# Hybrid mLSTM / gated-DeltaNet / HGRN2 step: the prompt's tokens first, then sample, then meta tokens, with fewer and narrower score and update matmuls

## The chip, the cores and the metric

The kernel runs on one core of one Trainium2 chip. The metric is device time in microseconds (us) of one execution. Five engines work from their own in-order queues: TensorE (PE in the profile, its weight loads PEld), VectorE (DVE), ScalarE (ACT), GpSimd (POOL), and SyncE (SP), which here issues every DMA.

## The reference

One layer of a decoder. A sequence of 1024 prompt tokens with 16 learned meta tokens ahead of it, and 8 sample sequences of 8 tokens, go through one wide projection; 16 heads of three kinds mix the tokens; a gated, head-normalised result goes through the output projection. The meta tokens are dropped from the output, but they leave a state behind (and a convolution history) on which the prompt goes on.

```python
proj = einsum('bld,de->ble', rmsnorm(x), w_in)      # 2048 -> 8984 columns
(aq, ak, av, ao, ai, af, bq, bk, bv, ba, bb, cq, cf, ci, z) = split(proj)
# 6 mLSTM heads (A), 6 gated-delta heads (B, with a width-4 convolution over q, k, v), 4 HGRN2 heads (C)
# HGRN2, inside a chunk: A[t,s] = sum_d q[t,d] k[s,d] exp(b[t,d] - b[s,d]),  s <= t, b = cumsum(log f)
#   o = (q exp(b)) S + A v ;  S' = exp(b_end) S + (k exp(b_end - b))^T v
y = concat(ha, hb, hc) * rsqrt(mean(.^2) + eps) * out_norm_w * silu(z)
out = x + einsum('ble,ed->bld', y, w_out);  y_prompt = rmsnorm(out[:, 16:]) * final_norm_w
```

Every float is 32 bits wide, and all states are outputs: those of the prompt, and those of the 8 sample sequences.

## The kernel before

**Two halves.** The tokens lie along the free axis. The first half (class `Half`, index 0) has 592 columns: 64 of the samples (`NSAMP`), 16 meta (together `NT0` = 80), and the first 512 of the prompt; the second half has the other 512. The normalised, transposed input is kept as pairs hi, lo of rounded floats (`hT`, tiles hA and hB in the profile); so is each piece of weights (`feed_split`: ACT makes `whi`, DVE makes `wlo` from `wraw`). A product is whi·hi + whi·lo + wlo·hi.

**Projection.** A head has 4 or 5 column tiles of 128 columns (`head_tiles`: q, k, v, the output gate o of an A head, z, and f of a C head). For each tile `run_group` goes over 16 blocks of the inner dimension, 3 products each; in the first half every product is two matmuls of 296 columns (`half.accs`, 592 / 2), in the second one of 512. The results are the tiles `acc`. All token columns are computed for every tile, those of the meta tokens too.

**Everything else is woven between these matmuls.** `Weave` holds queues of generators (scan, fin, post, bg); after each inner step `pump` lets those go on whose due time, by a table of assumed instruction costs (`Clock`), has come. Where a queue must be empty, at a new head or at the end of a half, `drain` runs the generators with no projection in between. The recorded program then passes a scheduler that also moves instructions on each engine.

**Heads.** `gate_scan` and `gates` make the gate rows of all A and B heads, write them to DRAM and read them back per head. `mlstm_scan`, `gdn_scan` and `hgrn_scan` work by chunks of 128 prompt tokens (`main`) and one small group of the 80 sample and meta tokens. In `hgrn_scan`, `score` fills the chunk's matrix `AT` level by level: first the diagonal (kT against qT), then for each block length hh of 1, 2, 4, 8 one matmul per chunk (tile `pa`) whose wanted entries a mask picks with a predicated copy; the last level takes hh = 16 for the whole chunk and puts hh = 32 and 64 over it with small matmuls of 32x32 and 64x64 (tile X of level 32, tile Ex of level 64). `sample_update` adds 8 outer products to the sample states of a head: keys as hi and lo (`kq`, 64 + 64 rows), values `vh` and `vl` spread by a row mask to 4 x 128 columns (`vx`), two matmuls of 512 columns (tile `pu`) for each half of the 8 sequences. In the first half `conv_evac` and `conv_post` load the 24 old rows of a B tile (tile `cr`), transpose them on PE (tile `pch`) and copy them into the convolution's input U, for each of the 18 tiles.

**Start.** `prep` normalises and transposes tiles of tokens: 0 (sample and meta, 80 rows), 1 and 2 (128 prompt rows each) ahead of the first matmul, 3 and 4 in the background of the first pass, which computes the first 296 columns of two tiles.

Of the kernel before, what the change touches and what calls it, by code (L numbers as in the profile page):

```python
# [28 lines left out]
WB = HALF  # L29
SUB = 16  # L30
# [16 lines left out]
class Half:  # L47
    def __init__(self, index):
        self.index = index
        self.first = index == 0  # L50
        self.width = WA if self.first else WB
        self.base = NT0 if self.first else 0
        self.tiles = ([(0, NT0)] if self.first else []) + [(self.base + P * c, P) for c in range(NC)]
        self.accs = [(0, WA // 2), (WA // 2, WA // 2)] if self.first else [(0, WB)]
        n0 = len(self.tiles) - NC
        self.main = Group(P, NC, self.base, n0, False)
        self.groups = ([Group(NT0, 1, 0, 0, True)] if self.first else []) + [self.main]
# [123 lines left out]
def hybrid_step(ctx, tc, i, o):  # L181
# [98 lines left out]
    def new_accs(half, cols):  # L280
        return [[bank("acc") for _ in half.accs] for _ in cols]

    def run_group(half, cols, accs, parts, after=None):
        for g in range(NG):
            for n in range(len(cols)):
                whi, wlo = next_piece()
                for q in range(4):
# [5 lines left out]
                    for w, part, first, last in products:  # L293
                        for a, (off, cnt) in list(zip(accs[n], half.accs))[parts]:
                            T.matmul(a[:, 0:cnt], w[:, cs], hT[g][part][:, q, off:off + cnt], start=first, stop=last)
# [6 lines left out]
    def spans(half, acc):  # L302
        return [(a[:, 0:cnt], off, cnt) for a, (off, cnt) in zip(acc, half.accs)]
# [49 lines left out]
    def load_x(n):  # L353
        xs = [row(("eghj" if n in (2, 3) else "abcd")[g], f"x{g}")[:, 0:512] for g in range(NG)]
# [32 lines left out]
    def prep(tiles):  # L387
        pend = []
        for n in tiles:
            cnt, col = (P, NT0 + P * (n - 1)) if n else (NT0, 0)  # L390
            xs = xtiles.pop(n) if n in xtiles else load_x(n)
            pend.append((xs, prep_stats(xs, cnt, n > 1), cnt, col, n > 1))
# [8 lines left out]
    xtiles = {0: load_x(0)}  # L401
# [8 lines left out]
    xtiles.update({n: load_x(n) for n in (1, 2)})  # L410
# [25 lines left out]
    xtiles.update({n: load_x(n) for n in (3, 4)})  # L436
# [5 lines left out]
    first_accs = new_accs(halves[0], first_cols)  # L442
# [85 lines left out]
    G.tensor_copy(imask, ident)  # L528
    rowmask = cp.tile([P, NB], F32, name="rowmask")
# [23 lines left out]
    hist = cp.tile([P, 3 * HB, 3], F32, name="hist")  # L553

# [58 lines left out]
    def gate_scan(half, acc):  # L613

        both = row("c", "both")
        for a, off, cnt in spans(half, acc):
            S.copy(both[:, off:off + cnt], a)
# [6 lines left out]
        for _, off, cnt in spans(half, acc):  # L624
# [6 lines left out]
    def gates(half, pre, li):  # L631
# [65 lines left out]
        DMA(rd[R_NM], M[RF])  # L697
        DMA(rd[R_EM], em[RF])
# [17 lines left out]
        for n, (c0, cnt) in enumerate(half.tiles):  # L716
# [39 lines left out]
    def finish(half, head, outs, ssq, scale, zs):  # L756
# [28 lines left out]
        for part, t in enumerate((yhi, ylo)):  # L785
            t = t.bitcast(F32)
            at_ = 2 * NSAMP if half.first else 0
            DMA(d[:, at_ + HALF * part:at_ + HALF * (part + 1)], t[:, half.base:half.base + HALF])
            if half.first:
                DMA(d[:, NSAMP * part:NSAMP * (part + 1)], t[:, 0:NSAMP])  # L790

    def sample_cols(t):
        return t[:, 0:NSAMP].rearrange("p (b x) -> p b x", x=NS)
# [44 lines left out]
    def sample_update(st, keys, vals, dec, dst, h):  # L838

        st = st[:, :, 0:P]  # L840
        G.tensor_tensor(st, st, dec.unsqueeze(2).to_broadcast([P, NB, P]), op=ALU.mult)
        k2, vl = (sp.tile([P, P], F32R, tag=t, name=t, bufs=1) for t in ("kq", "vl"))
        vh = sq("Wt", "vh", dtype=F32R)
        keys, vals = keys[0:NSAMP], vals[0:NSAMP, 0:P]
        S.copy(k2[0:NSAMP], keys)
        S.copy(vh[0:NSAMP], vals)
        S.copy(vh[NSAMP:P], vals)
        ck.sync()
# [3 lines left out]
        ck.sync()  # L852
# [13 lines left out]
    def mask_rows(half, t, m0, op, fill, strict):  # L866
        if half.first:
            V.tensor_tensor(t[:NT0, 0:NT0], t[:NT0, 0:NT0], m0[:NT0], op=op)
        v = half.main.cols(t)
        causal(v, v, fill, strict, reps=NC)  # L870


    def mlstm_scan(half, h, kT, qT, vT, tho, zs, nm, em, st):
        W = half.width
        mask_rows(half, nm, am0, ALU.add, NEG, False)
# [5 lines left out]
        G.tensor_tensor(qd[:, half.base:W], qT[:, half.base:W], em[:, half.base:W], op=ALU.mult)  # L881
# [44 lines left out]
        for g, kw, v1 in zip(half.groups, kws, v1s):  # L926
            if g.small:
# [6 lines left out]
                V.tensor_tensor(nu, nsv, em[:, NS - 1:NSAMP:NS], op=ALU.mult)  # L934
# [18 lines left out]
        for g, E, kw, v1, og in zip(half.groups, Es, kws, v1s, ogs):  # L953
            n = g.n
            hx = gt("5", g)
            for c0 in range(0, g.nt, 2):
                cs = list(range(c0, min(c0 + 2, g.nt)))
                nd = bank("nd")
                for c in cs:
# [5 lines left out]
                    T.matmul(dst, E[0:n, c, 0:n], v1[0:n, c], start=False, stop=True)  # L965
                ndv = nd[0:n, 0:256 * len(cs)].rearrange("p (c x) -> p c x", x=256)
# [10 lines left out]
            if g.small:  # L977
                upd = sample_update(st, kw[:, 0], v1[:, 0], em[:, NS - 1:NSAMP:NS], o["mC_s"], h)
            yield
            square_sums(g, hx[0:n], ssq)  # L980
# [9 lines left out]
    def conv_evac(half, acc, ei):  # L990
        U = row("u", "U")
        base = NB * (NS + 3)
        if half.first:
            us = U[:, 0:base].rearrange("p (b x) -> p b x", x=NS + 3)
            a0, a1 = acc
# [700 lines left out]
```

## Time and profile before

| what | value |
|---|---|
| median of 3 runs | 2583.55 us (2581.64 to 2584.42) |
| the profiled execution | 2583.26 us, of which the span from first to last instruction is 2581.6 us |
| busy in the span | PE 2525.8, DVE 1352.9, ACT 1010.8, POOL 534.9 us |
| mean granted TensorE clock | 0.994 |
| HBM traffic | 268.93 MB read, 45.42 MB written, 122 GB/s over the span |

The span and the time differ by 1.7 us, which lie outside the instructions. A busy share is a mean over stages; where the engines wait is in the rows further down.

### The profile page before, as it was taken

What the parts mean: (1) busy time and instruction counts of PE and PEld (TensorE: products, weight loads), DVE (VectorE), ACT (ScalarE), POOL (GpSimd) and SP (SyncE); (2) the same over time, 40 slices, a digit from 0 to 9 for tenths busy, and PEclk for the clock granted to TensorE, in tenths of its full rate; (3) what the DMA queues carried; (4) which work ended last, traced back from release to release, by engine and by line L of the source; (5) the groups of instructions that cost most, each with busy time, mean ns of one, the idle gap of its engine ahead of it and who ended that gap; (6) DMA issues with size and microseconds to landing.
All of it is one profiled execution on the core that took longest, in us unless ns stands there. A gap on an engine that the chain in (4) does not pass through costs nothing.

```text
span 2581.6 us, 43090 instructions
## 1 busy us (share of the span) xinstructions
PE 2525.8 (98%) x16084; PEld 2264.0 (88%) x16084; DVE 1352.9 (52%) x2811; ACT 1010.8 (39%) x2423; POOL 534.9 (21%) x665
## 2 busy tenths in 40 slices
PE   6899999999999999999999999999999999999998
PEld 5899999998999999999788888888888888888886
DVE  7664545654645654546764546455454545422435
ACT  5733334342334333334643434333433434322324
POOL 5231212320212321203230103110120101211201
PEclk9999999999999999999999999999999999999999
DMA  5633433555534333435543434334434447535735
GB/s 133 172 82 102 123 81 93 151 142 146 150 87 103 105 108 87 107 92 150 156 112 94 111 85 123 101 96 107 105 91 105 107 99 258 145 85 181 264 98 180
DMA packets 458461, 317.18 MB, mean 123 GB/s; under 512 B 56884, under 2 KB 402572, under 8 KB 457228
## 3 DMA queue, kind: packets, MB, share of 16 engines
q1 hardware_dynamic: 458252, 314.43, 45.1%
q8 instruction: 126, 2.06, 0.3%
q14 instruction: 83, 0.68, 0.1%
HBM read 268.93 MB, written 45.42 MB: 122 GB/s over the span
## 4 chain that ended last, share of the span: by engine, by line
PE 82%; issue 5%; DMA 5%; DVE 3%; POOL 2%; ACT 1%; SPq 1%; POOLq 0%; DVEq 0%; ACTq 0%
PE acc L127 60%; PE oacc L127 8%; PE pa L127 2%; PE pu L127 1%; PE po L127 1%; PE pz L127 1%; PE pyy L127 1%; DMA wraw<-in_w_in_dram 1%; PE nd L127 1%; DMA wraw<-in_w_out_dram 1%; POOL res L127 1%; PE poh L127 1%; POOL X L127 1%; DVE wlo L127 1%; DMA px<-in_x_prompt_dram 1%
## 5 line engine op out<-in xcount | busy, mean ns | idle before, releaser
L127 DVE TENSOR_TENSOR wlo<-wraw,whi 128x512 fp32r<-128x512 f32 x720 | 522.7, 729 | 622.4 <-ACT whi L127 604.8
L127 PE MATMUL acc<-hA,whi 128*128 128x296 f32 x4544 | 837.3, 307 | 8.1 <-ACT whi L127 6.9
L127 ACT CAST whi<-wraw 128x512 fp32r<-128x512 f32 x720 | 443.2, 619 | 937.3 <-PE acc L127 648.4
L127 PE MATMUL acc<-hB,whi 128*128 128x512 f32 x2272 | 722.5, 400 | 0.2 <-ACT whi L127 0.2
L127 PEld LDWEIGHTS acc<-hA,whi 128*128 128x128 f32 x4544 | 683.0, 191 | 16.1 <-ACT whi L127 9.2
L127 PE MATMUL acc<-hA,wlo 128*128 128x296 f32 x2240 | 494.5, 301 | 3.5 <-DVE wlo L127 3.5
L127 PEld LDWEIGHTS acc<-hB,whi 128*128 128x128 f32 x2272 | 408.6, 188 | 77.1 <-ACT whi L127 0.7
L127 PE MATMUL acc<-hB,wlo 128*128 128x512 f32 x1120 | 439.0, 392 | 1.2 <-DVE wlo L127 1.2
L127 PEld LDWEIGHTS acc<-hA,wlo 128*128 128x128 f32 x2240 | 367.4, 190 | 5.4 <-DVE wlo L127 5.3
L127 PE MATMUL oacc<-whi,y 128*128 128x512 f32 x1088 | 344.2, 391 | 0.7 <-ACT whi L127 0.7
L127 PEld LDWEIGHTS acc<-hB,wlo 128*128 128x128 f32 x1120 | 210.2, 188 | 48.9 <-DVE wlo L127 2.8
L127 PEld LDWEIGHTS oacc<-whi,y 128*128 128x128 f32 x1088 | 204.3, 188 | 44.2 <-ACT whi L127 2.4
L127 PE MATMUL oacc<-wlo,y 128*128 128x512 f32 x576 | 224.7, 390 | 0.9 <-DVE wlo L127 0.9
L127 PEld LDWEIGHTS oacc<-wlo,y 128*128 128x128 f32 x576 | 108.2, 188 | 24.5 <-DVE wlo L127 2.5
L127 POOL TENSOR_TENSOR res<-res,fnw 128x512 f32<-128x512 f32 (+1 forms) x34 | 54.3, 1625 | 259.2 <-ACT oscr L127 259.2
L127 POOL TENSOR_TENSOR qd<-qT,emb 128x512 f32<-128x512 f32 x12 | 15.5, 1290 | 361.9 <-PE po L127 288.6
L127 POOL TENSOR_TENSOR vx<-vh,rowmask 128x512 fp32r<-128x512 f32 x32 | 36.1, 1127 | 206.2 <-ACT vh L127 122.5
L127 POOL TENSOR_TENSOR y<-y,zs 128x592 fp32r<-128x592 f32 (+1 forms) x32 | 45.9, 1435 | 139.8 <-ACT zs L127 129.2
L127 DVE TENSOR_TENSOR Yt<-Yc,Bb 128x60 f32<-128x60 f32 (+8 forms) x180 | 36.6, 204 | 44.2 <-DMA Bb<-db 39.1
L127 POOL TENSOR_TENSOR X<-Ex,hk 128x256 f32<-128x256 f32 (+2 forms) x40 | 37.2, 931 | 104.0 <-PE pa L127 90.8
L127 PE MATMUL pa<-X 128*128 128x128 f32 (+2 forms) x480 | 57.8, 260 | 0.5 <-DVE AT L127 0.5
L127 PEld LDWEIGHTS pa<-X 128*128 128x128 f32 (+2 forms) x480 | 50.0, 165 | 9.2 <-issue 0.9
(401 smaller groups left out, 2784.7 us busy)
## 6 DMA issues: line engine op xcount, KB each, us to landing
wraw<-in_w_in_dram SPq DMA_DIRECT2D x564, 256.0 KB
wraw<-in_w_out_dram SPq DMA_DIRECT2D x144, 256.0 KB
y<-y SPq DMA_DIRECT2D x16, 576.0 KB
px<-in_x_prompt_dram SPq DMA_DIRECT2D x32, 256.0 KB
out_dram<-sst SPq DMA_DIRECT2D x16, 512.0 KB
y<-zs SPq DMA_DIRECT2D x32, 256.0 KB
y<-y SPq DMA_DIRECT2D x32, 256.0 KB
res<-in_x_prompt_dram SPq DMA_DIRECT2D x32, 256.0 KB
```

The costliest lines, as they stand in the source:

```text
L127: return f(out, *a, **k)
```

## The change

It does seven things. (1) The columns of the first half are put in the order prompt, sample, meta. (2) Tiles of which the meta tokens need no output (q of A and C heads, o of A heads, all z: 32 of the 71 tiles of the first half) leave the last 16 columns out: two matmuls of 288; the other tiles take 288 and 304. Their 16 columns are set to zero by POOL (`no_meta`). (3) `sample_update` takes four sequences (32 rows) at a time and stacks hi and lo of keys and values as four products in the 128 rows, so that one matmul of 512 columns is left where there were two. (4) `score_near` gets the diagonal and level 1 from one matmul of 192 columns per chunk (kT against `q3`, which holds q of both tokens of a pair and the decayed q of the second). (5) The small group has no level 8 matmul any more. (6) At the last level the four chunk matmuls come first, then the small ones, and those of hh = 64 are two of 32 rows. (7) The old convolution rows come in four loads of 108 rows through a background stream (`load_conv_states`) with four transposes, and POOL copies a tile's part into U. The start takes tiles 1, 2, 3 first, then 4 and 0.

```diff
-        self.accs = [(0, WA // 2), (WA // 2, WA // 2)] if self.first else [(0, WB)]
+    def accs(self, short):
+        if not self.first:
+            return [(0, WB)]
+        return [(0, WS // 2), (WS // 2, (WS if short else WA) - WS // 2)]
...
+        return [[(bank("acc"), off, cnt) for off, cnt in half.accs(what in ("o", "z") or what == "q" and name[0] != "B")]
+                for name, what, _ in group]
...
+    def no_meta(half, t):
+        if half.first:
+            G.memset(t[:, WS:WA], 0.0)
+        return t
...
-    xtiles = {0: load_x(0)}
+    xtiles = {1: load_x(1)}
...
-    for _ in prep([0, 1, 2]):
+    for _ in prep([1, 2, 3]):
...
-    weave.add("bg", prep([3, 4]))
+    weave.add("bg", prep([4, 0]))
...
+    def load_conv_states():
+        rows = 6 * 3 * HB
+        src = i["state_gdn_conv"][0].rearrange("b r (e c) -> (b r e) c", c=P)
+        crs = []
+        for g in range(4):
+            crs.append(sq("cr", "cr"))
+            DMA(crs[g][0:rows], src[rows * g:rows * (g + 1)])
+            ck.last = ck.t["T"] + 4.0
+            yield
+            pc = bank("pch")
+            T.transpose(pc[:, 0:rows], crs[g][0:rows], ident[0:rows, 0:rows])
+            V.tensor_copy(conv_states[:, 6 * g:6 * (g + 1)], pc[:, 0:rows].rearrange("p (q e) -> p q e", e=3 * HB))
...
-        k2, vl = (sp.tile([P, P], F32R, tag=t, name=t, bufs=1) for t in ("kq", "vl"))
-        vh = sq("Wt", "vh", dtype=F32R)
-        S.copy(k2[0:NSAMP], keys)
-        S.copy(vh[0:NSAMP], vals)
-        S.copy(vh[NSAMP:P], vals)
-        V.tensor_tensor(k2[NSAMP:P], keys, k2[0:NSAMP], op=ALU.subtract)
-        V.tensor_tensor(vl[0:NSAMP], vals, vh[0:NSAMP], op=ALU.subtract)
-        V.tensor_tensor(vl[NSAMP:P], vals, vh[0:NSAMP], op=ALU.subtract)
         for part in range(2):
+            rows = slice(32 * part, 32 * (part + 1))
+            k4, v4 = (sp.tile([P, P], F32R, tag=t, name=t, bufs=2) for t in ("k4", "v4"))
+            q = [slice(32 * x, 32 * (x + 1)) for x in range(4)]
+            for x in q[0:2]:
+                S.copy(k4[x], keys[rows])
+            for x in (q[part], q[2]):
+                S.copy(v4[x], vals[rows])
+            for x in q[2:4]:
+                V.tensor_tensor(k4[x], keys[rows], k4[rows], op=ALU.subtract)
+            for x in (q[1 - part], q[3]):
+                V.tensor_tensor(v4[x], vals[rows], v4[rows], op=ALU.subtract)
+            x = sp.tile([P, 4, P], F32R, tag=f"vx{part}", name="vx", bufs=1)
+            (G, V)[part].tensor_tensor(x, v4.unsqueeze(1).to_broadcast([P, 4, P]), quadmask.unsqueeze(2).to_broadcast([P, 4, P]), op=ALU.mult)
+            yield
             bs = slice(4 * part, 4 * part + 4)
-            vx = [sp.tile([P, 4, P], F32R, tag=f"vx{n}", name="vx", bufs=1) for n in range(2)]
-            for e, x, v in zip((G, V), vx, (vh, vl)):
-                e.tensor_tensor(x, v.unsqueeze(1).to_broadcast([P, 4, P]), rowmask[:, bs].unsqueeze(2).to_broadcast([P, 4, P]), op=ALU.mult)
-            yield
             pu = bank("pu")
-            for n, x in enumerate(vx):
-                T.matmul(pu, k2, x, start=n == 0, stop=n == 1)
+            T.matmul(pu, k4, x, start=True, stop=True)
...
                 for c in range(NC):
-                    T.matmul(pv[:, c], g.col(X, c), g.col(Y, c), start=True, stop=True)
+                    T.matmul(pv[:, c], g.col(X, c), g.col(X, c), start=True, stop=True)
+                for c in range(NC):
                     for X2, hh in sub:
                         x = g.col(X2, c)
-                        for b in range(0, P, 2 * hh):
-                            l, r = slice(b, b + hh), slice(b + hh, b + 2 * hh)
-                            T.matmul(pv[l, c, r], x[:, l], x[:, r], start=True, stop=True)
+                        for l in range(0, P, 32):
+                            b = l - l % (2 * hh)
+                            if l < b + hh:
+                                r = slice(b + hh, b + 2 * hh)
+                                T.matmul(pv[l:l + 32, c, r], x[:, l:l + 32], x[:, r], start=True, stop=True)
...
+        def score_near(q3):
...
+                    for c in cs:
+                        T.matmul(pa[:, c - c0], g.col(kT, c), v3[:, c], start=True, stop=True)
```

The scheduler's order shows where PE's work now stands. First, PE at the last score level of the first HGRN head (C0), before: `pa` is the score, X and Ex the tiles of the levels; a row is a run of like matmuls.

```order
L127 MATMUL acc<-hA_82,wlo 128x296 x2
L127 MATMUL pa<-X_1675 128x128
L127 MATMUL pa<-X_1717 32x32 x2
L127 MATMUL pa<-Ex 64x64
L127 MATMUL pa<-X_1675 128x128
L127 MATMUL pa<-X_1717 32x32 x2
```

PE at the same place after the change:

```order
L136 MATMUL acc<-hA_84,wlo 128x304
L136 MATMUL pa<-X_1742 128x128 x4
L136 MATMUL pa<-X_1782 32x32 x2
L136 MATMUL pa<-Ex 32x64 x2
L136 MATMUL pa<-X_1782 32x32 x2
L136 MATMUL pa<-Ex 32x64 x2
```

The change between full-width and narrow matmuls comes once for the four chunks instead of once for each.

Second, PE at the first mLSTM head (A0), before: from the scores (pst) over the transposes of k and v (pk, pv) to those of the gate (pot) and the state update (pum), with projection in between; py belongs to the head before.

```order
L127 MATMUL pst<-qT,kT 128x128 x4
L127 MATMUL acc<-hA_84,whi 128x296 x2
L127 MATMUL acc<-hA_85,whi 128x296 x2
L127 MATMUL acc<-hA_84,wlo 128x296 x2
L127 MATMUL acc<-hA_84,whi 128x296 x2
L127 MATMUL acc<-hA_85,whi 128x296 x2
L127 MATMUL acc<-hA_84,wlo 128x296 x2
L127 MATMUL acc<-hA_86,whi 128x296 x2
L127 MATMUL acc<-hA_87,whi 128x296 x2
L127 MATMUL acc<-hA_86,wlo 128x296 x2
L127 MATMUL pk<-ident,kT 80x128
```

PE at the same place after:

```order
L136 MATMUL pst<-qT,kT 128x128 x4
L136 MATMUL pk<-ident,kT 80x128
L136 MATMUL pv<-ident,vT 80x128
L136 MATMUL pk<-ident,kT 128x128 x4
L136 MATMUL pv<-ident,vT 128x128 x4
L136 MATMUL py<-ident,t_3414 128x80
L136 MATMUL py<-ident,s_3416 128x128 x4
L136 MATMUL pot<-ident,tho 80x128
L136 MATMUL pot<-ident,tho 128x128 x4
L136 MATMUL pum<-meta_725,kwall 128x137
L136 MATMUL pum<-s_3437,kwall 128x129 x4
L136 MATMUL nd<-sst,spread_722 32x129 x8
```

Here A0's steps stand one behind the other with no projection between them; the other five A heads of the first half keep most of theirs apart, as before.

## Rows read from the trace of the kernel before

**Rows 1.** The page, part 1: busy us, share of the span, instructions.
```profile
PE 2525.8 (98%) x16084; PEld 2264.0 (88%) x16084; DVE 1352.9 (52%) x2811; ACT 1010.8 (39%) x2423; POOL 534.9 (21%) x665
```
**Rows 2.** Busy time by stretch: a stretch of each half.
```profile
150.00:300.00 150.00, 150.00 (x1215) 145.85 (x1214) 77.97 (x191) 55.55 (x164) 33.88 (x43) 1.00 0.39 99
1300.00:1500.00 200.00, 200.00 (x1078) 166.89 (x1078) 100.47 (x205) 76.10 (x187) 33.88 (x36) 1.00 0.41 106
```
**Rows 3.** Who PE waited for: total us, times, longest us.
```profile
PE pt L127 <- DVE x L127: 14.1, 7, 6.3
PE acc L127 <- ACT whi L127: 7.1, 4, 3.4
```
**Rows 4.** PE's timeline, first half: start, length, instructions, count.
```profile
403.41 0.71 PE L127 MATMUL acc<-hA,whi 128*128 128x296 f32 x4
...
404.23 0.38 PE L127 MATMUL pr<-state_B,knT 128*128 128x128 f32 x2
```
**Rows 5.** PE's timeline, second half.
```profile
1505.04 0.61 PE L127 MATMUL acc<-hB,whi 128*128 128x512 f32 x2
...
1505.72 0.61 PE L127 MATMUL acc<-hB,whi 128*128 128x512 f32 x2
```
**Rows 6.** PE's timeline at one half of a sample update.
```profile
402.13 0.63 PE L127 MATMUL pu<-vx,kq 128*128 128x512 f32 x2
402.60 0.70 PE L127 MATMUL acc<-hA,whi 128*128 128x296 f32 x4
```
**Rows 7.** PE's timeline at the diagonal score of C1, first half.
```profile
487.15 0.43 PE L127 MATMUL acc<-hA,wlo 128*128 128x296 f32 x2
487.42 1.24 PE L127 MATMUL pa<-hq,hk 128*80 128x80 f32 x10
...
489.04 0.44 PE L127 MATMUL acc<-hA,wlo 128*128 128x296 f32 x2
```
**Rows 8.** PE's timeline at the diagonal score of C1, second half.
```profile
1593.13 0.39 PE L127 MATMUL acc<-hB,wlo 128*128 128x512 f32 x1
...
1594.71 0.39 PE L127 MATMUL acc<-hB,wlo 128*128 128x512 f32 x1
```
**Rows 9.** PE's timeline at level 8 of C2, first half.
```profile
883.07 0.44 PE L127 MATMUL acc<-hA,wlo 128*128 128x296 f32 x2
...
885.13 0.43 PE L127 MATMUL acc<-hA,wlo 128*128 128x296 f32 x2
```
**Rows 10.** PE's timeline at the last score level of C1, first half.
```profile
517.05 0.57 PE L127 MATMUL pa<-X 128*128 128x128 f32 x6
...
520.40 0.74 PE L127 MATMUL pvh<-ident,hvT 128*80 128x128 f32 x5
```
**Rows 11.** PE's groups by shape: busy us, mean ns, idle before.
```profile
L127 PE MATMUL pa<-X 128*32 128x32 f32 x128 | 8.2, 207 | 0.0
```
**Rows 12.** PE's timeline at a transpose of old convolution rows.
```profile
295.02 0.43 PE L127 MATMUL acc<-hA,wlo 128*128 128x296 f32 x2
295.38 0.24 PE L127 MATMUL pch<-ident,cr 24*128 24x24 f32 x1
...
296.20 0.43 PE L127 MATMUL acc<-hA,wlo 128*128 128x296 f32 x2
```
**Rows 13.** PE's timeline: the one such transpose that waited.
```profile
691.60 0.21 PE L127 MATMUL pch<-ident,cr 24*128 24x24 f32 x1 [1.77 <-DMA cr<-in_state_gdn_conv_dram]
```
**Rows 14.** Busy time by stretch, around that wait (PEclk is the granted clock).
```profile
685.00:700.00 15.00, 13.23 (x87) 12.95 (x87) 8.17 (x17) 4.57 (x10) 4.27 (x6) 0.89 0.74 208
```
**Rows 15.** PE's timeline: first and last step of A0's scan.
```profile
278.73 1.24 PE L127 MATMUL pst<-qT,kT 128*80 128x80 f32 x10
...
290.54 0.97 PE L127 MATMUL nd<-sst,spread 128*32 128x129 f32 x14
```
**Rows 16.** Groups by shape: one cast of values on ACT.
```profile
L127 ACT CAST vh<-t 64x128 fp32r<-64x128 f32 x20 | 6.0, 298 | 0.4
```

More of the change, by code (lines that the diff above doesn't have):

```diff
@@ L293, in run_group @@
                     for w, part, first, last in products:
-                        for a, (off, cnt) in list(zip(accs[n], half.accs))[parts]:
+                        for a, off, cnt in accs[n][parts]:
                             T.matmul(a[:, 0:cnt], w[:, cs], hT[g][part][:, q, off:off + cnt], start=first, stop=last)
@@ L302, in spans @@
     def spans(half, acc):
[L303 removed]
+        return [(a[:, 0:cnt], off, cnt) for a, off, cnt in acc]
+    def no_meta(half, t):
+        if half.first:
+            G.memset(t[:, WS:WA], 0.0)
+        return t
     def head_groups(half):
@@ L353, in load_x @@
     def load_x(n):
-        xs = [row(("eghj" if n in (2, 3) else "abcd")[g], f"x{g}")[:, 0:512] for g in range(NG)]
+        xs = [row(("eghj" if n in (3, 4) else "abcd")[g], f"x{g}")[:, 0:512] for g in range(NG)]
         for g in range(NG):
@@ L409, in hybrid_step @@
         V.tensor_copy(nwb[g], pn)
-    xtiles.update({n: load_x(n) for n in (1, 2)})
+    xtiles.update({n: load_x(n) for n in (2, 3)})
     prows = sq("io", "prows")
@@ L528, in hybrid_step @@
     G.tensor_copy(imask, ident)
+    quadmask = cp.tile([P, NB // 2], F32, name="quadmask")
+    G.memset(quadmask, 1.0)
+    for r in range(0, P, 32):
+        v = quadmask[r:r + 32]
+        G.affine_select(v, v, pattern=[[-NS, NB // 2]], compare_op=ALU.is_ge, fill=0.0, base=0, channel_multiplier=1)
+        G.affine_select(v, v, pattern=[[NS, NB // 2]], compare_op=ALU.is_ge, fill=0.0, base=NS - 1, channel_multiplier=-1)
     rowmask = cp.tile([P, NB], F32, name="rowmask")
@@ L616, in gate_scan @@
         for a, off, cnt in spans(half, acc):
-            S.copy(both[:, off:off + cnt], a)
+            n = min(cnt, HALF - off)
+            S.copy(both[:, half.base + off:half.base + off + n], a[:, 0:n])
+            if n < cnt:
+                S.copy(both[:, 0:NT0], a[:, n:cnt])
         sel = sq("io", "sel")
@@ L623, in gate_scan @@
         pre, li = row("a", "pre")[:, 0:half.width], row("d", "li")[:, 0:half.width]
-        for _, off, cnt in spans(half, acc):
+        for off, cnt in half.accs(False):
             a = bank("gsum")[:, 0:cnt]
@@ L696, in gates @@
         rd = rows_dram[half.index]
-        DMA(rd[R_NM], M[RF])
-        DMA(rd[R_EM], em[RF])
+        for n, t in ((R_NM, M), (R_EM, em)):
+            DMA(rd[n][:, 0:HALF], t[RF, half.base:W])
+            if half.first:
+                DMA(rd[n][:, HALF:W], t[RF, 0:NT0])
         yield
@@ L715, in gates @@
         cols_of[half.index] = cols
-        for n, (c0, cnt) in enumerate(half.tiles):
+        for n, (c0, cnt) in enumerate(half.gtiles):
             pc = bank("pc")
@@ L864, in sample_update, with mask_rows @@
         DMA(dst[0, :, h].rearrange("b d e -> d b e"), st)
[L866 to L869, printed above, removed]
+    def mask_rows(gs, t, m0, op, fill, strict):
+        if gs[0].small:
+            v = gs[0].col(t, 0)[:NT0]
+            V.tensor_tensor(v, v, m0[:NT0], op=op)
+        v = gs[-1].cols(t)
         causal(v, v, fill, strict, reps=NC)
@@ L1324, in score @@
                 if g.small:
-                    if lo0 is None:
-                        continue
-                    r = slice(lo0, NT0)
-                    T.matmul(pa[r, r], X[:, r], Y[:, r], start=True, stop=True)
-                    V.copy_predicated(at0[r, r], mask0[r, r], pa[r, r])
+                    if small:
+                        r, x = slice(0, NT0), g.col(X, 0)
+                        T.matmul(pa[r, r], x, x, start=True, stop=True)
+                        V.copy_predicated(at0[r, r], mask[r, r], pa[r, r])
                     continue
@@ L1341, in hgrn_scan @@
+        q3 = sp.tile([P, 3 * WA // 2], F32, tag="q3", name="q3", bufs=1)
+        qp = q3[:, 0:3 * W // 2].rearrange("p (m x) -> p m x", x=3)
+        G.tensor_copy(qp[:, :, 0:2], qT[:, 0:W].rearrange("p (m x) -> p m x", x=2))
         yield
-        score(kT, qT, imask, imask, 0)
         Xs = {}
         for hh in LEVELS:
-            lo0 = 0 if hh <= 4 else (NSAMP if hh == 8 else None)
-            lo = (NT0 if lo0 is None else lo0) if half.first else 0
+            hi = W if hh <= 4 else HALF
@@ L1559, in hybrid_step @@
             else:
-                accs = new_accs(half, cols)
+                accs = new_accs(half, group)
                 run_group(half, cols, accs, slice(0, 2), after)
```

145 lines of the change are left out of this document (85 added, 60 removed).

## The prediction

> **What bounds the kernel now.** The page's first part comes first: PE is busy for 2525.8 of 2581.6 us, DVE for about half, ACT for 39% [rows 1]. The windows by stretch then say whether this mean hides stages with another limit. In 150 to 300 us and in 1300 to 1500 us PE is busy from end to end, at full granted clock, and nothing else is near [rows 2]. So what is taken from PE's stream shortens the time one for one, as long as the other engines' results still come in time. The view of waits says how near they are to being late: against 2525.8 busy us [rows 1] even its two largest entries are small, 14.1 us for x at the start and 7.1 us for the whi pieces [rows 3].
>
> Busy figures mislead about prices, since matmuls overlap: a 296-column one is listed at about 0.3 us. I therefore use the distance between starts. Six of 296 columns take 404.23 - 403.41 = 0.82 us, 0.137 each [rows 4]; three of 512 take 0.68 us, 0.227 each [rows 5]. The difference is 0.090 us for 216 columns, 0.417 ns a column. A block of scores or transposes is priced in the same way: the distance between projection starts around it, less the projection matmuls in it.
>
> **The change, part by part.** All sums are against the profiled execution, 2583.3 us, which is 0.3 us from the median of the runs.
>
> (a) Narrow tiles. 32 tiles x 16 blocks x 3 products x 16 columns = 24,576 columns less; x 0.417 ns = 10.2 us [rows 4, 5]. The split into 288 and 304 costs nothing where the price is linear.
>
> The Trainium skill speaks against this term ("TensorE: Matmul & The Clock Gate", section "Back-to-back issue gap"): in streams of weight load and matmul pairs the spacing is set by both, about 81 ns at 128 columns and 131 at 512. That is 0.13 ns a column, by which the term would be an estimated 3.2 us and the time 2551. This trace disagrees with that rule, with 137 ns at 296 columns and 227 at 512.
>
> (b) Sample updates. Two matmuls of 512 in 402.60 - 402.13 = 0.47 us become one [rows 6]: 0.235 x 32 (16 heads, two parts) = 7.5 us. The price is four casts and four subtractions for each part. ACT gets 128 casts for 48; even at the old 0.30 us [rows 16] that is 24 us on an engine 39% busy [rows 1]. The split of the weights on ACT is what PE could come to wait for; so far that is 7.1 us in all [rows 3]. POOL's spreads halve.
>
> (c) Diagonal and level 1 in one. First half: 489.04 - 487.15 = 1.89 us with six projection matmuls (0.82), so 1.07 for ten passes, eight of 128 columns and two of 80 [rows 7]; two such levels are 2.14. Second half: 1.58 - 3 x 0.227 = 0.90 for eight passes, 0.112 each [rows 8]; two are 1.80. Now a pass has 192 columns, 0.168 if linear: 8 x 0.168 = 1.34, and two of 120 about 0.25. Saved are 0.54 and 0.46, for four heads each 4.0 us together. Bounds 3 and 5, for the changes of tile around it.
>
> (d) Level 8 of the small group. 885.13 - 883.07 = 2.06, less 0.82 and less 0.90 for the main chunks: 0.35 x 4 heads = 1.4 us [rows 9].
>
> (e) The last level. It takes 520.40 - 517.05 = 3.35 us now [rows 10]. The four chunk matmuls by themselves are 0.90 [rows 8]. A chunk's small ones have 32 + 64 columns in two passes, 0.17 at the pace of rows 8; before, 0.84 - 0.23 - 0.17 = 0.44 us a chunk went into three changes of shape. With strips of 32 all through, neighbouring ones can run at once: 128 matmuls of 32 x 0.207 = 26.5 us lie in 8.2 us [rows 11]. I take 0.27 a chunk, its columns and 0.10 for a change that shows, and 0.2 for the way back: 0.90 + 1.08 + 0.2 = 2.18, saved 1.17 x 8 = 9.4 us. Bounds: 13.4 if all changes are hidden (0.90 + 0.17 x 4 + 0.1), 3.9 if two changes a chunk still show (0.47 a chunk and 0.08).
>
> (f) Old convolution rows. A transpose with its surroundings: 296.20 - 295.02 = 1.18, less 0.82: 0.36 x 18 = 6.5; four larger ones at about 0.11 remain, so 6.0 us [rows 12]. Their four loads lie on SP's queue in the background. The 18 copies into U go to POOL, 21% busy [rows 1], in front of the convolutions of the same tile.
>
> (g) The wait of one such transpose for its load, 1.8 us [rows 13], and the lower clock right behind it, 15 x (1 - 0.89) = 1.7 us [rows 14]: 3.5 us. All four loads are now issued before the first B tile is done, so that the wait has no counterpart.
>
> Gains: 10.2 + 7.5 + 4.0 + 1.4 + 9.4 + 6.0 + 3.5 = 42.0 us.
>
> **What it costs.** By the new order the gate scan stands later against the projection, so A0 starts later, and its steps stand one behind the other at a drain. Before, they ran from 278.73 to about 290.5 [rows 15], 11.8 us with 54 projection matmuls (7.4 us) in between. These were what PE did while DVE and ACT made the next operand. Between nothing (inputs ready anyway) and all 7.4 us, I take 2: rows from other steps of the heads rarely show PE waiting [rows 3], but here the steps depend on one another. The start loads a tile of 128 rows first in place of 80 rows, where PE waited for DVE [rows 3]: DVE works on partitions side by side, so little changes for a tile, but 12 transposes in place of 12 with fewer rows and four more background loads may cost 1 us. The zeroing of 16 columns on POOL is small, beside work that is 21% busy. The wider last columns of the gate rows (two DMAs more) are queued on SP before reads with the same lead as before: nothing, else up to 1 us.
>
> Sum: 2583.3 - 42.0 + 3 = 2544.
>
> **Rivals.**
> *Columns don't pay.* If weight loads paced PE, 288 columns would take what 296 do. For it: PEld is busy 145.85 of 150 us [rows 2]. Against it: in the second half it is 166.89 of 200, and starts are 0.137 and 0.227 apart [rows 4, 5]; loads that paced would make them alike. With (a) at 3 or less: 2551. Chance 0.07. The Trainium skill's section named above ("TensorE: Matmul & The Clock Gate", "Back-to-back issue gap") would put the time there too.
> *Strips don't run side by side.* (e) gives 3.9: 2550. For it: weights have to change for each strip. Against it: rows 11. Chance 0.12.
> *All changes of shape hidden, no drain cost*: 2583.3 - 46 - 1 + 1 = 2537. Chance 0.06.
> *The scans come late.* The drain of A0 costs all its 7.4 us (5.4 over what I took) and a second head in the first half as much: 2544 + 12.8 = 2557. For it: the scans stand 10 to 60 projection matmuls later through A0. Against it: by A1 the order has caught up, and DVE has half its time free [rows 2]. Chance 0.12.
> *Slower: the stacked update comes late.* Before its matmul there are now four casts, four subtractions and a spread in a chain: at 0.30 us [rows 16] 2.4 us ahead of the spread, where six such steps fed both parts. The matmul is issued in order, so the projection behind it waits too. From 42 / 32 = 1.3 us uncovered for each of 32 the gain is gone; at 1.6 us each (51 us) the time is 2595. Against it: 30 to 54 projection matmuls stand ahead of each such matmul since its step began, 4 to 7 us. Chance 0.03.
> *Nothing gained*, because several waits eat it: 2583. Chance 0.02.
>
> **How the numbers follow.** The forecast has 0.58, with 2538 to 2551 its own range. Rivals on the gaining side reach from 2537 to 2557. All favourable bounds together (4 for e, 1 for c, 3 for the losses) give 2536, all unfavourable ones (5.5, 1, 5.4) 2556; with some 2 us for what runs scatter the range is 2534 to 2559, which leaves out the last two rivals and the worst of the late scans. A measurement of this kernel tells about 0.2% (5 us) from no change. Faster 0.95, same 0.02, slower 0.03.
>
> **What would show it right or wrong.** In PE's timeline, starts of short tiles 0.133 us apart, of the wider part 0.140 (a); one pu matmul of about 0.235 in each part and no wait on vx, k4 or v4 (b); one block of diagonal and level 1 of about 1.34 in the second half (c); the last level 2.2 us long (e); four pch transposes and no wait for cr (f, g). At A0 a row of scan steps without projection, with idle time in brackets: their sum is the price of the drain. PE's busy time should fall by about 37 us and its idle time little. The forecast is wrong if PE's waits for whi, wlo or vx rise to tens of us, if the granted clock drops in new places behind such waits, or if the last level stays near 3 us.

## The result, and the profile after

The changed kernel takes 2549.95 us (median of 4 runs, 2546.89 to 2551.2) against 2583.24 us of the kernel before: a ratio of 0.987, 95% interval 0.9853 to 0.9887. That is 33.3 us saved, where 39 were forecast (2544, range 2534 to 2559). Run again on another occasion it took 2551.01 us (0.9876, 0.9863 to 0.9889). The profiled execution was the fastest of the four, with a span of 2545.2 us; the second time the span was 2549.5 us.

The page's first part, which answers to [rows 1]:

```profile
span 2545.2 us, 43177 instructions
PE 2482.4 (98%) x16022; PEld 2226.0 (87%) x16022; DVE 1376.3 (54%) x2881; ACT 1024.0 (40%) x2512; POOL 552.8 (22%) x722
```

PE has 43.4 us less to do, where the forecast's signs had about 37. The span less PE's busy time, its idle time, was 2581.6 - 2525.8 = 55.8 us and is now 62.8 (65.5 the second time). So the work went down as forecast, and a little more, and about 7 to 10 us of it came back as waits. The view of waits, in the order of its columns total, times and longest, shows which (answers to [rows 3]):

```profile
PE pt L136 <- DVE x L136: 12.0, 8, 6.6
PE acc L136 <- ACT whi L136: 11.6, 12, 2.1
PE acc L136 <- DVE whi L136: 4.8, 2, 3.9
PE nd L136 <- DVE s L136: 4.1, 3, 1.4
```

The start's wait for x is a little shorter, though the first projection matmul comes 1.1 us later (32.62 us for 31.51); that for the weight pieces is longer (7.1 before), 4.8 for DVE's copy in the gate piece are new (0.8 before), and nd, the read-out of an mLSTM head, waits three times.

The steps one by one, in PE's timeline. Short tiles: six projection matmuls of 288 columns, 401.21 - 400.42 = 0.79 us (0.82 for six of 296 in [rows 4]).

```profile
400.42 0.69 PE L136 MATMUL acc<-hA,whi 128*128 128x288 f32 x4
400.95 0.42 PE L136 MATMUL acc<-hA,wlo 128*128 128x288 f32 x2
401.21 0.38 PE L136 MATMUL pw<-s,s 128*128 128x128 f32 x2
```

The sample update: one matmul, 183.52 - 183.29 = 0.23 us, where [rows 6] had 0.47.

```profile
183.29 0.40 PE L136 MATMUL pu<-vx,k 128*128 128x512 f32 x1
183.52 0.70 PE L136 MATMUL acc<-hA,whi 128*128 128x288 f32 x4
```

Diagonal and level 1 in one (tile pan), second half: 1566.07 - 1564.07 = 2.00 us with three projection matmuls, 2.00 - 3 x 0.227 = 1.32, where two blocks of 0.90 stood, 1.80 together [rows 8].

```profile
1564.07 0.40 PE L136 MATMUL acc<-hB,wlo 128*128 128x512 f32 x1
1564.31 1.47 PE L136 MATMUL pan<-q,hk 128*128 128x192 f32 x8
1565.47 0.76 PE L136 MATMUL acc<-hB,whi 128*128 128x512 f32 x2
1566.07 0.39 PE L136 MATMUL acc<-hB,wlo 128*128 128x512 f32 x1
```

The last level of C1: 507.76 - 505.96 = 1.80 us, where [rows 10] had 3.35.

```profile
505.96 1.21 PE L136 MATMUL pa<-X 128*128 128x128 f32 x10
...
507.76 0.64 PE L136 MATMUL pvh<-ident,hvT 128*80 128x128 f32 x4
```

A0's scan, where [rows 15] spread the steps over 11.8 us: they now run without projection in between, from 282.06 to 288.02, and the time lost in this stretch is some two tenths of a microsecond, ahead of the pum of 285.73.

```profile
282.06 1.24 PE L136 MATMUL pst<-qT,kT 128*80 128x80 f32 x10
...
285.28 0.40 PE L136 MATMUL pum<-meta,kwall 80*128 80x137 f32 x2
285.73 1.13 PE L136 MATMUL pum<-s,kwall 128*128 128x129 f32 x8
...
288.02 0.81 PE L136 MATMUL acc<-hA,whi 128*128 128x288 f32 x4
```

What the forecast overlooked is A1 and the other four mLSTM heads of this half: they too run from py to nd without projection, where only one did before, and in three of them the read-out waits. The wait of A1:

```profile
432.59 0.46 PE L136 MATMUL nd<-s,qd 128*128 128x129 f32 x2 [1.41 <-DVE s L136]
```

### The profile page after: what moved, and what is told of

The parts are those of the page before. It is cut to its first block, busy times and chain, and to the rows that moved or that the text cites. A ratio compares the mean times of both kernels' runs of the same rounds, so it can differ in the third digit from the quotient of the medians.

```text
span 2545.2 us, 43177 instructions
## 1 busy us (share of the span) xinstructions
PE 2482.4 (98%) x16022; PEld 2226.0 (87%) x16022; DVE 1376.3 (54%) x2881; ACT 1024.0 (40%) x2512; POOL 552.8 (22%) x722
## 4 chain that ended last, share of the span: by engine, by line
PE 80%; issue 5%; DMA 4%; DVE 4%; POOL 3%; ACT 2%; SPq 0%; POOLq 0%; DVEq 0%; ACTq 0%
PE acc L136 59%; PE oacc L136 8%; PE pa L136 1%; DVE wlo L136 1%; PE po L136 1%; PE pyy L136 1%; PE pz L136 1%; POOL res L136 1%; PE pu L136 1%; PE nd L136 1%; POOL X L136 1%; DMA wraw<-in_w_in_dram 1%; PE poh L136 1%; DMA wraw<-in_w_out_dram 1%; DMA x<-in_x_prompt_dram 1%
## 5 line engine op out<-in xcount | busy, mean ns | idle before, releaser
L136 DVE TENSOR_TENSOR wlo<-wraw,whi 128x512 fp32r<-128x512 f32 x720 | 534.2, 746 | 639.4 <-ACT whi L136 628.3
L136 PE MATMUL acc<-hA,whi 128*128 128x288 f32 (+1 forms) x4544 | 822.9, 303 | 16.1 <-ACT whi L136 10.1
L136 PEld LDWEIGHTS acc<-hA,whi 128*128 128x128 f32 x4544 | 675.4, 190 | 23.2 <-ACT whi L136 12.3
L136 PE MATMUL acc<-hA,wlo 128*128 128x288 f32 x2240 | 487.9, 298 | 0.2 <-DVE wlo L136 0.2
L136 PEld LDWEIGHTS acc<-hB,whi 128*128 128x128 f32 x2272 | 408.8, 188 | 79.7 <-ACT whi L136 3.4
L136 POOL TENSOR_TENSOR hr<-hr,halfneg 128x4 f32<-128x4 f32 (+1 forms) x48 | 47.2, 984 | 56.0 <-DVE hr L136 55.0
L136 POOL TENSOR_TENSOR X<-Ex,hk 128x256 f32<-128x256 f32 (+1 forms) x40 | 38.5, 963 | 93.2 <-PE pa L136 75.5
L136 POOL TENSOR_TENSOR nrm<-nrm,halfneg 128x10 f32<-128x10 f32 x12 | 23.5, 1956 | 129.3 <-DVE nrm L136 129.3
L136 DVE TENSOR_TENSOR Sx<-Sx,lf 128x256 f32<-128x256 f32 (+2 forms) x60 | 34.0, 569 | 26.9 <-ACT Ex L136 24.9
```

Source lines behind the costliest of these rows:

```text
L136: return f(out, *a, **k)
```

## The experiments

All are edits of the changed kernel. Medians stand in the table, with the ratio to the kernel before on the same chip; PE's busy time and the span less it are those of the profiled execution.

| run | median us | ratio, 95% interval | PE busy | rest of span |
|---|---|---|---|---|
| changed kernel | 2549.95 | 0.9870 (0.9853, 0.9887) | 2482.4 | 62.8 |
| after_again | 2551.01 | 0.9876 (0.9863, 0.9889) | 2484.0 | 65.5 |
| e1_wide | 2552.84 | 0.9885 (0.9872, 0.9899) | 2491.2 | 59.3 |
| e2_oldlevel | 2565.32 | 0.9934 (0.9921, 0.9946) | 2496.2 | 67.3 |
| e3_oldupdate | 2549.96 | 0.9877 (0.9863, 0.9890) | 2489.3 | 63.4 |
| e4_oldconv | 2562.41 | 0.9925 (0.9912, 0.9939) | 2492.8 | 67.8 |
| e5_oldnear | 2545.20 | 0.9851 (0.9836, 0.9866) | 2486.3 | 60.6 |
| e6_order64 | 2560.05 | 0.9910 (0.9896, 0.9924) | 2489.9 | 65.6 |
| e7_clock | 2568.22 | 0.9946 (0.9934, 0.9958) | 2486.8 | 79.7 |
| e8_allold | 2583.60 | 0.9999 (0.9991, 1.0008) | 2520.3 | 58.4 |
| e9_clock_oldupdate | 2581.47 | 0.9994 (0.9985, 1.0003) | 2500.0 | 83.7 |
| e10_clock_wide | 2576.27 | 0.9970 (0.9958, 0.9982) | 2496.2 | 75.8 |
| e12_wide_oldupdate | 2568.35 | 0.9947 (0.9934, 0.9959) | 2500.3 | 66.3 |

**One saving undone at a time.** The short tiles:

```diff
-        return [[(bank("acc"), off, cnt) for off, cnt in half.accs(what in ("o", "z") or what == "q" and name[0] != "B")]
+        return [[(bank("acc"), off, cnt) for off, cnt in half.accs(False)]
```

> The changed kernel with one part undone: every tile of the first half takes 288 and 304 columns (24,576 columns more). Theory: a column costs 0.417 ns, so about 10 us are given back, some 2560 us (ratio to the kernel before 0.991). Rival 1, weight loads pace PE: at most 3 us given back, 2550 to 2553. Rival 2, the narrow tiles also took cover from the scans: less than 8 us given back, and PE's waits on DVE's score tiles (nd) in the first half, 4.1 us in the changed kernel, are gone.

PE has 8.8 us more to do (7.2 against after_again), so columns pay; but only 2.9 us come back (1.8), and PE's other time falls by 3.5 (6.2). With four executions on each side such a difference is uncertain by some 3 us. The waits at nd are down to 0.6 us, and those for whi from 11.6 to 8.2:

```profile
PE acc L136 <- ACT whi L136: 8.2, 9, 2.5
PE nd L136 <- DVE s L136: 0.6, 1, 0.6
```

This is the second rival: what a short tile takes from PE it also takes from the time that other engines had for their results.

The last level:

```diff
-                        for l in range(0, P, 32):
-                            b = l - l % (2 * hh)
-                            if l < b + hh:
-                                r = slice(b + hh, b + 2 * hh)
-                                T.matmul(pv[l:l + 32, c, r], x[:, l:l + 32], x[:, r], start=True, stop=True)
+                        for b in range(0, P, 2 * hh):
+                            l, r = slice(b, b + hh), slice(b + hh, b + 2 * hh)
+                            T.matmul(pv[l, c, r], x[:, l], x[:, r], start=True, stop=True)
```

This is e6_order64, where the four full matmuls still come first; e2_oldlevel also puts a chunk's full matmul and its small ones back into one loop.

> The changed kernel with the last score level as it was: per chunk the full matmul, then two of 32x32 and one of 64x64. Theory: a block of 3.3 us instead of about 2, eight of them, 9 to 11 us given back, 2559 to 2561. Rival, strips of 32 do not run side by side: 4 us given back, 2554.

> The changed kernel with the four chunk matmuls first at the last level, but level 64 as one matmul of 64x64 for each chunk. The block took 3.34 us before and takes 1.80. Theory of the prediction: both the order and the strips count, 2.6 us a block, 2556. Rival 1, the order alone does it (only the step between full width and narrow costs): 1.9 to 2.1 us, 2552. Rival 2, the strips alone: 3.1 us or more, 2561.

The whole part is worth 15.4 us, the strips alone 10.1 of them and the order the other 5.3; e6_order64's four executions lie between 2556.8 and 2563.3 us, so this split is uncertain by some 3 us. The blocks split it more sharply. With the old last level the block takes 3.34 us (e2_oldlevel; 3.35 in [rows 10]). In e6_order64 it takes 510.98 - 508.23 = 2.75 us, between 3.34 and 1.80: both count, and the strips count more. The time follows the blocks (8 x 1.54 = 12.3 us, of which 0.95 x 8 = 7.6 by strips) with 2 to 3 us on top. Nearly one price fits all three: 0.90 for the chunk matmuls, 4 x 0.17 for the columns of the small ones, and what is left for each change of shape. Before, there are three a chunk, 12 in a block, and 3.34 - 1.58 = 1.76 us is left, 0.147 each; in e6_order64 there are nine, and 1.17 is left, 0.130 each; in the changed kernel two, and 0.22 is left, 0.11 each. That the strips of 32 run side by side is in the same numbers: a chunk's eight passes have 384 columns, 0.34 us one behind the other at 0.875 ns a column, and all that the small ones take in the changed kernel is 0.90 / 4 = 0.225 us, changes of shape included.

```profile
508.23 1.24 PE L136 MATMUL pa<-X 128*128 128x128 f32 x12
509.39 0.33 PE L136 MATMUL pa<-Ex 128*64 128x64 f32 x2
509.65 0.26 PE L136 MATMUL pa<-X 128*32 128x32 f32 x4
...
510.98 0.74 PE L136 MATMUL pvh<-ident,hvT 128*80 128x128 f32 x5
```

The sample update:

```diff
-            T.matmul(pu, k4, x, start=True, stop=True)
+            for n, x in enumerate(vx):          # vx from vh and vl, k2 from keys hi and lo
+                T.matmul(pu, k2, x, start=n == 0, stop=n == 1)
```

> The changed kernel with the sample update as it was: two matmuls of 512 columns for each four sequences, 48 casts on ACT in place of 128. Theory: 32 x 0.235 = 7.5 us given back, 2557, and PE's waits for whi unchanged. Rival, the casts make the weight pieces late: 4 us or less given back, because PE's waits for whi (11.6 us in the changed kernel, 7.1 before) fall.

No time comes back, with 6.9 us more on PE. The waits for whi are what they were (11.1), so the casts are not the reason. Nor did the stacked form's chain of casts and subtractions hold PE up: in the changed kernel its matmul waits once, 1.2 us. The old form's own waits are larger, 3.4 us for POOL's spread, and the wlo pieces are later:

```profile
PE acc L136 <- DVE wlo L136: 7.8, 12, 1.6
PE pu L136 <- POOL vx L136: 3.4, 3, 1.2
```

The profile of this run is its slowest execution (2554.4 us), 3 to 8 us above those of the changed kernel, while the medians are level. The interval of the ratio leaves some 3 us on either side, so the forecast 7.5 us are hardly compatible with it.

The convolution rows:

```diff
-            G.tensor_copy(us[:, :, 0:3], conv_states[:, :, ei].rearrange("p (b r) -> p b r", r=3))
+            cr = sq("io", "cr")
+            DMA(cr[0:3 * NB, :], i["state_gdn_conv"][0, :, :, P * ei:P * (ei + 1)].rearrange("b r c -> (b r) c"))
...
+            T.transpose(pc[:, 0:3 * NB], cr[0:3 * NB, :], ident[0:3 * NB, 0:3 * NB])
```

> The changed kernel with the old convolution rows as they were: a load and a transpose for each of the 18 tiles. Theory: 6.0 us of PE given back, 2556; the load wait of 1.8 us comes back for one tile at most, with or without the clock's dip (another 3.5). Rival: the background stream only moved the cost to POOL's copies, under 3 us given back.

12.5 us come back. PE waits for the load not once but three times, 5.2 us. PE's busy time rises by 10.4 us (8.8 against after_again), more than the 6.0 of the transposes: behind the longest wait the granted clock is at its lower level, as it was in [rows 14], and matmuls take longer there (four of 288 columns last 1.19 us in PE's timeline, elsewhere 0.70). So the clock's dip that the prediction counted in (g) is back as well.

```profile
PE pch L136 <- DMA cr<-in_state_gdn_conv_dram: 5.2, 3, 3.0
```

```profile
680.00:690.00 10.00, 8.71 (x43) 8.69 (x44) 5.58 (x11) 1.93 (x3) 1.63 (x3) 0.66 0.70 202
```

Diagonal and level 1 apart:

```diff
-            if hh == 1:
-                score_near(q3)
+        score(kT, imask, True, Y=qT)        # ahead of the levels; level 1 then as levels 2 to 8
```

> The changed kernel with the diagonal and level 1 as two sets of matmuls of 128 columns. Blocks were 1.08 and 1.08 in the first half and 0.90 and 0.90 in the second; the joint one takes 1.51 and 1.31. Theory: 4.5 us given back, 2554 to 2555. Rival: DVE's two predicated copies for each half of the chunks and POOL's copy of q cost as much elsewhere, 0 to 2 us.

Neither: it is the fastest kernel measured, 2545.2 us, 5 us below the changed one, though the two intervals still touch (0.9836 to 0.9866 against 0.9863 to 0.9889 of after_again) and its span of 2546.9 us lies between the two of the changed kernel. The blocks do cost more (PE 2486.3 us), but the rest of the span, 60.6 us, is 2 to 5 us shorter. That joining these levels saves 4.5 us is refuted; that it costs time is likely, not shown. From 1230 us to the end of the second half, the waits of the changed kernel and then of this one are (two rows of each):

```profile
PE acc L136 <- DVE wlo L136: 2.0, 5, 0.6
PE acc L136 <- ACT whi L136: 1.5, 3, 0.8
```

```profile
PE acc L136 <- ACT whi L136: 0.8, 1, 0.8
PE acc L136 <- DVE wlo L136: 0.2, 1, 0.2
```

The joint form has the weight pieces late in the second half, 3.5 us of waits for 1.0; in the kernel before, with both sets of matmuls, it was 0.8. DVE and POOL have more to do in the joint form (1376.3 against 1366.9 us, 552.8 against 536.9); which of their steps makes the pieces late was not tested apart, and these 2.5 us do not account for the whole difference.

**All savings undone.** What is left are the token order, the start and the missing level 8.

> The changed kernel with all the savings undone: wide tiles, old last level, old sample update, old convolution rows, diagonal and level 1 apart. Left are the new order of the tokens, the new start and the small group's missing level 8. Theory: only these cost, 1 us at the start and 1 elsewhere less 1.4 for level 8, 2583 to 2585; all drains but one are gone with the savings. Rival: the order costs 5 to 10 us of its own (later scans), 2588 to 2593.

2583.6 us, the same as the kernel before (1.3 us, and its interval is 2 us to either side). So the order and the start, with the 1.4 us of level 8 added back, cost at most some 3.5 us together, which the prediction's 3 and its expectation's 2 both fit, and the savings as a whole are worth 2583.6 - 2550 = 33.6 us in this plan. Undone singly, they were worth 2.9, 15.4, nothing, 12.5 and -4.8, 26 us in sum. Each of the five is uncertain by some 3 us, so this shortfall alone would not show that they don't add up; the pair undone together further down shows it.

**Do rows of scan steps without projection cost time?** The planner (`Weave`) lets a scan go on by the projection it has issued, at a price for each matmul. With less work elsewhere between the same projection, six heads come to a drain where one did.

```diff
-                return max(0.107, n * 0.000422)
+                return 0.0125 + n * 0.000417
```

> The changed kernel once more, as the measure for the three beside it. Theory: 2550, ratio 0.987, and a profile with PE idle for about 50 us in all, 4 us of it before nd at the A heads, and execution times that scatter by some 4 us with the granted clock.

> The changed kernel with one number of the planner changed: a projection matmul is put at 12.5 ns plus 0.417 ns a column, as the trace shows it, where the table had 0.422 ns a column and nothing fixed. By the new order no A head of the first half runs from py to nd without projection any more (six of six did, one before the change). Theory, drains take back a part of the gain: PE's waits at nd (4.1 us) and in the row of scan steps are gone, 4 to 6 us faster than the changed kernel, 2544 to 2546, ratio 0.985. Rival: the waits only move, to px, whi or pu, 2549 to 2551.

The theory fell. The drains are gone, and so are nd's waits, but the kernel is 17 to 18 us slower than the changed one. By stretch (busy time of PE, PEld, DVE, ACT, POOL; first half, second half, output), the changed kernel and then this one:

```profile
32.00:1191.00 1159.00, 1132.53 (x9030) 1110.58 (x9031) 686.55 (x1556) 489.33 (x1315) 295.85 (x420) 0.99 0.45 117
1191.00:2143.00 952.00, 945.10 (x5164) 783.31 (x5163) 500.04 (x1023) 382.81 (x891) 164.11 (x179) 1.00 0.44 117
```

```profile
32.00:1195.00 1163.00, 1136.16 (x9033) 1116.49 (x9034) 684.67 (x1552) 493.30 (x1312) 287.75 (x418) 0.98 0.45 116
1195.00:2164.00 969.00, 946.22 (x5160) 783.27 (x5159) 510.96 (x1026) 388.69 (x895) 167.34 (x180) 1.00 0.43 115
```

The first half, where all the drains were, takes as long without them (1163 us against 1159, and 1162 in after_again), with 26.8 us of idle time for PE against 26.5: other waits have come for nd's, among them one of 5.0 us at a py of 661 us. So what the drains cost by themselves is not told apart from what the new plan costs here.

Nearly all the loss is in the second half, 969 us against 952, with 22.8 us of idle time for PE against 6.9. There px (the transposes inside the gated-delta scans) and py (those of a finished head's result) wait for DVE, 16 us in all (0.9 in the changed kernel):

```profile
PE px L136 <- DVE s L136: 10.0, 5, 3.1
PE py L136 <- DVE s L136: 6.0, 6, 1.8
```

They are issued with less projection ahead of them. Where the changed kernel has 75 projection matmuls between pvb and px, and 15 between pcn (a transpose for the next head's convolution) and py, this one has 69 and 3 (at 1355 and 1415 us, and at 1362 and 1424 us). The old price is too low, 0.216 us for the 512 columns that take 0.227 [rows 5], and that was slack: it put more of PE's time in front of each dependent step than the planner knew. This reading fits the two plans; no run tested it apart.

**Undone without the drains.** The same two savings, where the plan has no drains on either side:

> As the run with the planner's price mended, and the sample update as it was before the change. Undoing the update in the changed kernel itself cost nothing (2549.96), though PE had 6.9 us more to do. Theory, the drains hid it: without drains on either side the old update costs 6 to 8 us more than the mended kernel. Rival, the stacked update's own chain costs what its matmuls save: 0 to 2 us.

> As the run with the planner's price mended, and all tiles of the first half at 288 and 304 columns. Undoing the narrow tiles in the changed kernel cost 2.9 us, though PE had 8.8 us more to do. Theory, wider tiles gave back cover: without drains on either side they cost 8 to 10 us more than the mended kernel. Rival, columns hardly pay: 3 us.

> The changed kernel with wide tiles and the old sample update both. Each alone cost 3 us and nothing, with six, and three to five rows of scan steps without projection; together, by the new order, only one such row is left, as before the change. Theory, the two share the cover: PE's work of both, 8.8 and 6.9 us, less the 3 us of waits in these rows: 2561 to 2563. Rival: they add up as they did alone, 2553. Second rival: the interplay is plain scatter of the plan, anywhere up to 2570.

Against e7_clock the old update costs 13.3 us, more than the forecast 6 to 8, and the wide tiles 8.1, as forecast. Both together, with the planner's old price, cost 18.4 us, against 2.9 and nothing when undone singly. PE's busy time is additive: 2500.3 is 17.9 us above the changed kernel (16.3 above after_again), and 8.8 + 6.9 = 15.7. What isn't is the rest of the span, 66.3 us, where e1_wide had 59.3 and e3_oldupdate 63.4: together, PE's added work comes through as time, and singly most of it did not. The largest rise is in the waits for wlo (2.2 in the changed kernel), as it was with the old update alone:

```profile
PE acc L136 <- DVE wlo L136: 8.4, 9, 2.5
```

Whether drains eat the savings is left open. For it: in the plan without them the two savings are worth 8.1 and 13.3 us. Against it: e7_clock's first half is no faster without them, and e12_wide_oldupdate, which has one such row as the kernel before, is slower by 18.4 us, where the theory had 11 to 13; the second rival, plain scatter of the plan, covers that too. So which waits a plan draws is left without a simple rule. What the runs show is its size: up to 9 us between what a single saving was forecast to give and what it gave (e5_oldnear), and 17 us from the planner's price alone, more than any saving here.

## Why the prediction was right, and where its sum was off

**What bounds the kernel.** PE, as forecast: its busy time fell by 43.4 us in the profile, by 41.8 in the second, for a predicted 38.5 of terms (a) to (f) and 1.7 of clock. That the sum came within 6 us is in part luck. Undone singly, no saving gave in time what its term said: (e) gave 6 us more, (f) and (g) together 3 more, (a), (b) and (c) 7 to 9 less each, and these errors partly cancel.

**(a) Narrow tiles, 10.2.** Six matmuls of 296 took 0.82 us, six short ones take 0.79. Undone, PE has 8.8 us more. The rival that columns don't pay is out. The Trainium skill's rule ("TensorE: Matmul & The Clock Gate", section "Back-to-back issue gap") does not hold for this stream: by its figures the term would be an estimated 3.2 us of PE's time. The time gained by this part alone was 2.9 us, for another reason, waits; it was 8.1 us in the plan of e7_clock.

**(b) Updates, 7.5.** On PE 0.47 became 0.23 us, and 6.9 us in all. In the time nothing is to be seen alone, and 13.3 us in the plan of e7_clock. The rival that the longer chain is late is out: one wait of 1.2 us.

**(c) Diagonal and level 1, 4.0.** The block is smaller as worked out (1.32 for 1.80 in the second half), and PE has 3.9 us less to do, but no time is gained by it: by the medians the kernel is 5 us slower, likely and not shown. The step that failed is the silent one that its work on DVE and POOL is free: the waits for weight pieces in the second half are 2.5 us longer with it. That this work is the reason, and where the rest comes from, is not shown.

**(d) Level 8 and the start.** e8_allold puts these with the new order at 1.3 us in all, within its interval the forecast's 1.6 (3 less 1.4).

**(e) The last level, 9.4.** Mis-sized: 12.3 us in the blocks, near the upper bound of 13.4, and 15.4 in the time. A chunk's small matmuls cost 0.225 us, little above the 0.17 of their columns, not 0.27: after the change of order and strips only two changes of shape are left in a block. The step that failed is the 0.10 a chunk for "a change that shows": with strips of 32 for both levels there is none between them. The Trainium skill ("TensorEngine Tiling (Array Packing)", section "Key Properties") says that a change of the tiling mode drains TensorE, while tiles of one mode work independently; the three blocks agree, at 0.11 to 0.15 us a change. The rival that strips don't run side by side is out, by the pace of the small matmuls above. The forecast's own ground against it, 26.5 us of durations within 8.2 us [rows 11], would not have been enough: in the same trace the full-width matmuls of pa, of which none is a strip, also overlap (320 of 285 ns in 49.6 us).

```profile
L127 PE MATMUL pa<-X 128*128 128x128 f32 x320 | 49.6, 285 | 0.5 <-DVE AT L127 0.5
```

**(f), (g) Convolution rows, 6.0 and 3.5.** 12.5 in the time for 9.5. The waits for these loads are not a fixed 1.8 us but a matter of where the load falls: 5.2 us in e4_oldconv, with the lower clock behind the longest one, and 2.1 in e8_allold.

**The losses, 3.** This is the step that was too small. A0's drain cost 0.2 us and not 2, and the start 1.1. But PE's idle time rose by 7 to 10 us where 1.2 was forecast (3 less the 1.8 of g): 4 at nd in heads that the forecast held to be as before, 4 to 6 for whi, 4 for DVE's copy at the start, less some 2 each for x, for the convolution rows and for wlo. So the gains were larger than their sum by some 3 us, the losses by 6 to 9, and 33 came out for 39. The rival that the scans come late described the place (two heads losing their cover) but put a price of 7.4 us on each; three of them cost 1.4 each.

## What to carry to other kernels

Where one engine is busy from end to end, price its instructions by the distance between their starts: in PE's busy time the terms (a) to (c) held within a fifth, and the change of tile shape needed a run of its own. Then don't take the sum for the time: a microsecond that leaves the bounding engine also leaves the cover of what is woven into it, and each edit draws a new plan, which here moved the time by up to 9 us, and by 17 where only the planner's price was changed. An edit that saves the bound engine little and adds steps on the engines that feed it (here the joint near levels) is worth undoing once by itself.

## What the hardware showed that was not expected

A change of tile shape in PE's stream costs 0.11 to 0.15 us in the last level here (above). The old convolution transposes point the same way: one of 24 rows costs 0.36 us with its surroundings [rows 12], one of 108 rows in the changed kernel 60.72 - 60.33 = 0.39 us less two matmuls of 0.14, or 0.11. That a change of shape is the reason there was not tested.

```profile
60.33 0.26 PE L136 MATMUL pch<-ident,cr 108*128 108x108 f32 x1
60.36 0.52 PE L136 MATMUL acc<-hA,whi 128*128 128x304 f32 x2
60.72 0.30 PE L136 MATMUL acc<-hA,wlo 128*128 128x304 f32 x1
```

A granted clock in the view of stretches has to be checked against the pace of the matmuls. From 20 to 30 us the view gives 1.00 for the changed kernel and 0.55 for after_again (PE, PEld, DVE, ACT, POOL busy, granted clock, DMA share, GB/s), with the same busy time:

```profile
20.00:30.00 10.00, 6.98 (x28) 5.04 (x27) 8.60 (x17) 5.98 (x12) 0.99 (x1) 1.00 0.46 108
```

```profile
20.00:30.00 10.00, 6.98 (x28) 5.04 (x27) 8.60 (x17) 5.99 (x12) 0.99 (x1) 0.55 0.43 102
```

PE's timeline shows the level. First the changed kernel, then after_again:

```profile
17.89 1.12 PE L136 MATMUL pt<-ident,x 128*128 128x128 f32 x4 [2.38 <-DVE x L136]
25.94 2.79 PE L136 MATMUL pt<-ident,x 128*128 128x128 f32 x12 [0.35 <-DVE x L136]
```

```profile
17.90 0.66 PE L136 MATMUL pt<-ident,x 128*128 128x128 f32 x4 [2.40 <-DVE x L136]
25.94 2.79 PE L136 MATMUL pt<-ident,x 128*128 128x128 f32 x12 [0.35 <-DVE x L136]
```

Twelve transposes take 2.79 us in both, so both ran at the same level, 1.2 GHz, from 26 to 29 us, and the 1.00 is no measurement: in the changed kernel's trace the record of the clock begins only at 37 us. Where the levels did differ, at 17.9 us, four transposes took 1.12 us in the changed kernel and 0.66 in after_again. This cost nothing, as both kernels start their projection at 32.62 us.

Executions of one kernel scatter by some 4 us. The spans of these two differ by 4.3 us, and later stretches show a difference in the clock, 0.96 against 0.92 from 50 to 140 us:

```profile
50.00:140.00 90.00, 80.58 (x556) 77.59 (x556) 61.35 (x148) 55.74 (x122) 33.41 (x72) 0.96 0.65 157
```

```profile
50.00:140.00 90.00, 80.09 (x541) 78.00 (x540) 58.83 (x139) 55.86 (x122) 32.91 (x71) 0.92 0.66 155
```

By estimate 0.04 of 90 us are 3.6 us of full clock; how much of them became time is not shown.
